# Expert weights in 19 fixed slots, loaded by one, two and four tiles, and the last expert finished as rows

## The chip, the cores and the metric

The kernel runs on one core of one Trainium2 chip. The metric is the device time of one execution in microseconds. Before the change it is 2363.58 us, the median of 3 runs (2362.69 to 2364.72).

## The reference

Two transformer blocks work on the same 512 tokens of width 1024. The first is a retention block with a convolutional FFN. The second is a gated-MLP and window-attention block that ends in an expert-choice FFN and a final norm. Nearly all of the change lies in that FFN and that norm:

```python
def expert_choice_ffn(h, w_router, w_gate, w_up, w_down):      # 16 experts, D = 1024, D_EXPERT = 2048
    logits = jnp.einsum('bnd,de->bne', h, w_router)
    aff = jax.nn.softmax(logits, axis=-1)
    top_w, top_idx = lax.top_k(jnp.swapaxes(aff, 1, 2), cap)   # each expert takes cap = 64 of 512 tokens
    xe = jax.vmap(lambda hb, ib: hb[ib])(h, top_idx)
    g = jnp.einsum('becd,edf->becf', xe, w_gate)
    u = jnp.einsum('becd,edf->becf', xe, w_up)
    y = jnp.einsum('becf,efd->becd', jax.nn.silu(g) * u, w_down)
    y = y * top_w[..., None].astype(y.dtype)
    ... # add each y to its token
# second_block:  x = x + g2 * expert_choice_ffn(h2, ...);  return rmsnorm(x, final_g)
```

All values are float32. The three weight matrices of an expert are 24 MiB, those of 16 experts 384 MiB.

## The kernel before

The first three fifths of the span compute the first block and the attention part of the second with dense matmuls, whose weights are split into a high and a low part (lines 222 to 224). The expert phase comes after them; there the weights are used as they are.

**Tiles and their order.** The 24 MiB of one expert are 24 tiles of 1 MiB, each 128 partitions by 2048 floats, a row of 8 KB in every partition. Each tile is one contiguous piece of the input `w_exp` of shape (16, 24, 128, 2048). Tiles 0 to 7 hold gate and up weights of the first half of the hidden width (`j = 0`), 8 to 15 those of the second (`j = 1`), 16 to 23 the down weights. TensorE takes four matmuls for each tile (line 1733 for gate and up, 1791 for down), with the expert's 64 tokens as the stationary operand. The tiles are numbered through, expert e beginning at 24e, so the last is 383.

**Buffers.** 22 tiles are loaded ahead (`FIRST`, `ORDER`, line 1448). 17 of them lie in rotating buffers of three pools (`xw0` 9, `xw1` 2, `xw2` 6), which are the ring that all later tiles go round. Two lie in ring buffers of the dense part (kind 4), and one each in `xw3`, in small buffers of the norms (kind 5), and in `hTe` with two more (kind 6). `XOUT` says how many of them are issued at which of the eight output columns of the last dense product; the last eight follow when the dense buffers are closed (`dense_stack.close()`).

**Loads.** `x_dma_to` (line 1464) issues one load of 1 MiB per tile on SyncE's queue. `x_ahead(used)` is called after every tile that TensorE's code has used, and issues each load whose buffer's former tile is below `used`. Each load waits on the chip for the last matmul on that buffer.

**Between the tiles.** In expert e, during `j = 0`, the 64 output rows of expert e-1 are added into the 512 rows of the residual (`scatter`, line 1690: a one-hot matmul into a bank `ps`, then VectorE adds it into `xacc`). After every second expert the tokens of the next two are gathered (line 1666).

**The end.** For expert 15 the down weights lie in another order: tiles 376 to 379 hold the first 512 output columns and 380 to 383 the second 512. `down` (line 1819) runs them one half after the other; between its tiles an identity matmul (line 1835) copies the residual's second half into four banks. The first half's rows are scaled (`scaled`, line 1827) and scattered (line 1841) after four of the eight tiles, the second half's after the last (line 1854). Then ScalarE squares and sums each row (line 1858), `rsqrt_` (line 326) gives the norm, the rows are scaled (lines 1868, 1869), and eight stores of 256 KB each (line 1871) write the output.

Of the kernel before, what the change touches and what calls it, by code (L numbers as in the profile page):

```python
# [9 lines left out]
F32 = mybir.dt.float32  # L10
# [7 lines left out]
L = 512  # L18
# [24 lines left out]
def block_kernel(ctx: ExitStack, tc: tile.TileContext, A, out):  # L43
# [307 lines left out]
    class SumSq:  # L351
        def __init__(self, n, tag):
# [181 lines left out]
    def ctx_norm(cx, cH, cL, a, b):  # L534

        ss = SumSq(256, "c")
# [30 lines left out]
    c1 = ctx_norm(cx, cH, cL, A1[:, :, 1:2], mod1[:, 0:8, 1:2])  # L567
# [487 lines left out]
    for j in range(HID):  # L1055
# [404 lines left out]
    def x_dma_to(n):  # L1460
        while wn["d"] < min(n, len(wq)):
            i = wn["d"]
            at = ORDER[i] if i < NFIRST else i
            e, t = wq[at]
            g = FIRST[i if i < NFIRST else RING[(i - NFIRST) % NRING]]
            src = A["w_exp"][e, t]
            if g > 3:
                if g == 4:
                    w = [b.bitcast(F32) for _ in range(2) for b in ring(True)]
                elif g == 5:  # L1470
                    w = soon + [mp.tile([128, L], F32, name="xf", tag="ssqa", bufs=1)]
                else:
                    h = xp.tile([128, 2, L], F32, name="hTe", tag="hTe", bufs=1)
                    w = [h[:, 0], h[:, 1]] + [mp.tile([128, L], F32, name="xf", tag="t2", bufs=2) for _ in range(2)]
                for c in range(3 if g == 5 else 0, 4):
                    nc.sync.dma_start(w[c], src[:, c * 512:(c + 1) * 512])
            else:
                w = xws[g].tile([128, 2048], F32, name=f"xw{g}", tag="xw", bufs=FIRST.count(g))
                for c in (slice(0, 1024), slice(1024, 2048)) if i == len(wq) - 1 else (slice(0, 2048),):
                    nc.sync.dma_start(w[:, c], src[:, c])  # L1480
                w = [w[:, c:c + 512] for c in range(0, 2048, 512)]
            wt[at] = w
            wn["d"] += 1
# [23 lines left out]
    xws.append(ctx.enter_context(tc.tile_pool(name="xw1", bufs=1, side="right")))  # L1507
# [13 lines left out]
    XOUT = (3, 4, 5, 6, 8, 10, 12, 13)  # L1521
# [20 lines left out]
    def epi_out2(j, ps):  # L1542
# [158 lines left out]
    fg = []  # L1701

    def final_gain(hf):
# [5 lines left out]
        fg.append(mp.tile([128, 512], F32, name="fg", tag="ssqb" if hf else "ssqa", bufs=1))  # L1709
        nc.vector.tensor_copy(fg[hf], p)  # L1710

    turns_e = []
    for e in range(NEXP):
# [10 lines left out]
        for j in range(2):  # L1724
            pgu = [pbank("pgu", 3), pbank("pgu", 3)]
            for n in range(8):
# [51 lines left out]
        S = mp.tile([128, L], F32, name="S", tag="nh", bufs=2).bitcast(F32R)  # L1778
        nc.vector.tensor_scalar(S, iota, sw[:, e:e + 1], None, OP.is_equal)
        if e == NEXP - 1:  # L1780
            final_gain(1)
            break
# [13 lines left out]
        if e == 0:  # L1796
# [3 lines left out]
            g2L = yp.tile([128, 2, 512], F32, name="g2L")  # L1800
# [6 lines left out]


    ssf = xp.tile([128, 2, 4], F32, name="ssf")
    nc.scalar.activation(ssf[:, 0, 0:1], ones, AF.Sqrt)  # L1810
    vf = xp.tile([128, 2, 4], F32, name="vf")

    def down(py, q):
        t = wt.pop(ti + q)
        for n in range(4):
            f = q % 4 * 4 + n
            rows = slice(64 * (n % 2), 64 * (n % 2) + 64)
            c = f % 4 * 128 + f // 4 % 2 * 64
            nc.tensor.matmul(py[rows, :], hTe[:, f // 8, c:c + 64],  # L1819
                             t[n], start=f < 2, stop=f > 13, skip_group_check=True)  # L1820
        x_ahead(ti + q + 1)

    def scaled(py, hf):
        yh = yp.tile([128, 512], F32R, name="yh", tag="yh", bufs=1)
        y32 = mp.tile([128, 512], F32, name="y32", tag="nh", bufs=2)
        yl = yp.tile([128, 512], F32R, name="yl", tag="yl", bufs=1)
        nc.vector.scalar_tensor_tensor(y32, py, sw[:, 31:32], g2L[:, hf], OP.mult, OP.mult)
        split(yh, yl, y32)
        return yh, yl
    py = [pbank("py", 2) for hf in range(2)]  # L1830
    xlast = []
    for q in range(4):
        down(py[0], q)
        xlast.append(pbank("pT", 1) if q == 3 else pbank("pgu", 3))
        nc.tensor.matmul(xlast[q], ident, xacc[q][1], start=True, stop=False)
    ys = scaled(py[0], 0)
    down(py[1], 4)
    for t in range(4):
        p = pbank("ps", 2)
        for y in ys:  # L1840
            nc.tensor.matmul(p, S[:, t * 128:(t + 1) * 128], y, start=y is ys[0], stop=y is ys[1])
        x = xacc[t][0]
        nc.vector.tensor_tensor(x, p, x, OP.add)
        sq = mp.tile([128, 512], F32, name="sqf", tag="t2", bufs=2)
        nc.scalar.activation(sq, x, AF.Square, accum_out=ssf[:, 0, t:t + 1])  # L1845
        nc.gpsimd.tensor_tensor(x, x, fg[0], OP.mult)  # L1846
    nc.vector.tensor_scalar(vf[:, 0], ssf[:, 0], 1.0 / D, EPS, OP.mult, OP.add)
    down(py[1], 5)
    down(py[1], 6)
    down(py[1], 7)  # L1850
    ys = scaled(py[1], 1)
    for y in ys:
        for t in range(4):
            nc.tensor.matmul(xlast[t], S[:, t * 128:(t + 1) * 128], y, start=False, stop=y is ys[1])
    def squares(ts):
        for t in ts:
            sq = mp.tile([128, 512], F32, name="sqf", tag="t2", bufs=2)
            nc.scalar.activation(sq, xlast[t], AF.Square, accum_out=ssf[:, 1, t:t + 1])

    def last_rms(g):  # L1860
        ts = slice(2 * g, 2 * g + 2)
        nc.vector.scalar_tensor_tensor(vf[:, 1, ts], ssf[:, 1, ts], 1.0 / D, vf[:, 0, ts], OP.mult, OP.add)
        return rsqrt_(vf[:, 1, ts], 2, "f" if g else "x")

    def finish(g, rf):
        for i in range(2):
            t = 2 * g + i
            nc.scalar.activation(xacc[t][0], xacc[t][0], AF.Copy, scale=rf[:, i:i + 1])
            nc.vector.scalar_tensor_tensor(xacc[t][1], xlast[t], rf[:, i:i + 1], fg[1], OP.mult, OP.mult)
            for hf in range(2):  # L1870
                nc.sync.dma_start(out[t * 128:(t + 1) * 128, hf * 512:(hf + 1) * 512], xacc[t][hf])
# [159 lines left out]
```

## Time and profile before

| | us |
|---|---|
| median of 3 runs | 2363.58 |
| the profiled execution | 2362.11 |
| its span, first to last instruction | 2360.3 |
| TensorE matmul busy in the span | 2237.4 |
| expert phase, from the first matmul of line 1733 | 1423.5 to 2360.3 |

The span is what the profile shows; the profiled execution's own time is 1.8 us longer. "PE" is TensorE, "DVE" VectorE, "ACT" ScalarE, "POOL" GpSimd and "SP" SyncE, which issues most loads. "DMA share" is the mean busy share of the core's 16 DMA engines; it can come out a little above 1. [...]

### The profile page before, as it was taken

What the parts mean: (1) busy time and instruction counts of PE and PEld (TensorE: products, weight loads), DVE (VectorE), ACT (ScalarE), POOL (GpSimd) and SP (SyncE); (2) the same over time, 40 slices, a digit from 0 to 9 for tenths busy, and PEclk for the clock granted to TensorE, in tenths of its full rate; (3) what the DMA queues carried; (4) which work ended last, traced back from release to release, by engine and by line L of the source; (5) the groups of instructions that cost most, each with busy time, mean ns of one, the idle gap of its engine ahead of it and who ended that gap; (6) DMA issues with size and microseconds to landing.
All of it is one profiled execution on the core that took longest, in us unless ns stands there. A gap on an engine that the chain in (4) does not pass through costs nothing.

```text
span 2360.3 us, 28316 instructions
## 1 busy us (share of the span) xinstructions
PE 2237.4 (95%) x11052; PEld 1441.4 (61%) x11052; DVE 1062.8 (45%) x2059; ACT 658.0 (28%) x1033; POOL 173.5 (7%) x318
## 2 busy tenths in 40 slices
PE   9999999999999999999999999999898989898987
PEld 6888888878888887888876874434232323232322
DVE  4645775778787865436467551221111111111112
ACT  5632234354243454322566321000000000000002
POOL 0201001101112010004211000000000000000000
PEclk9999999999999999999999999999999999999999
DMA  8646345734566443347410788999999999999996
GB/s 316 241 162 202 99 138 179 241 122 143 165 189 219 143 148 107 92 127 178 101 41 6 234 350 346 420 420 420 421 420 421 420 420 421 420 420 420 420 421 277
DMA packets 128725, 616.56 MB, mean 261 GB/s; under 512 B 16464, under 2 KB 21200, under 8 KB 79248
## 3 DMA queue, kind: packets, MB, share of 16 engines
q1 hardware_dynamic: 109200, 557.59, 61.3%
q0 software_dynamic: 19392, 57.17, 8.5%
q8 instruction: 87, 1.43, 0.2%
q14 instruction: 46, 0.38, 0.0%
HBM read 590.05 MB, written 14.68 MB: 256 GB/s over the span
## 4 chain that ended last, share of the span: by engine, by line
PE 53%; DMA 30%; ACT 2%; DVE 2%; issue 1%; POOL 0%; SPq 0%; DVEq 0%; ACTq 0%; POOLq 0%
DMA xw<-in_w_exp_dram 27%; PE mm L224 10%; PE mm L222 10%; PE mm L223 10%; PE pgu L1733 6%; PE py L1791 3%; PE sm L1358 1%; PE mm L1346 1%; PE ps L1666 1%; PE pT L1666 1%; PE py L1819 1%; DMA qS<-rh 1%; PE b L1309 1%; PE b L255 1%; PE b L253 1%
## 5 line engine op out<-in xcount | busy, mean ns | idle before, releaser
L1733 PE MATMUL pgu<-xw,xt 128*64 128x512 f32 x2032 | 480.6, 601 | 56.8 <-DMA xw<-in_w_exp_dram 52.6
L222 PE MATMUL mm<-aH,wh 128*128 128x512 f32 (+1 forms) x1104 | 420.1, 381 | 2.3 <-ACT aH L380 2.3
L224 PE MATMUL mm<-aH,wl 128*128 128x512 f32 (+1 forms) x1104 | 417.3, 378 | 1.0 <-DVE wl L131 1.0
L223 PE MATMUL mm<-aL,wh 128*128 128x512 f32 (+1 forms) x1104 | 417.5, 378 | 0.0
L1733 PEld LDWEIGHTS pgu<-xw,xt 128*64 128x64 f32 x2032 | 131.3, 136 | 354.9 <-issue 199.2
L131 DVE TENSOR_TENSOR wl<-wraw,wh 128x1024 fp32r<-128x1024 f32 (+1 forms) x212 | 256.2, 1212 | 177.3 <-ACT wh L122 177.1
L122 ACT ACTIVATE wh<-wraw 128x1024 fp32r<-128x1024 f32 (+1 forms) x212 | 220.0, 1044 | 254.0 <-PE mm L223 180.3
L222 PEld LDWEIGHTS mm<-aH,wh 128*128 128x128 f32 x1104 | 208.5, 189 | 40.8 <-ACT aH L380 2.6
L224 PEld LDWEIGHTS mm<-aH,wl 128*128 128x128 f32 x1104 | 208.4, 189 | 40.4 <-DVE wl L131 1.8
L1791 PE MATMUL py<-xw,hTe 128*64 128x512 f32 x944 | 214.7, 597 | 19.1 <-DMA xw<-in_w_exp_dram 19.1
L223 PEld LDWEIGHTS mm<-aL,wh 128*128 128x128 f32 x1104 | 208.5, 189 | 38.0 <-DVE aL L383 0.4
L1791 PEld LDWEIGHTS py<-xw,hTe 128*64 128x64 f32 x944 | 65.0, 136 | 157.4 <-issue 111.0
L1761 DVE TENSOR_TENSOR eg<-pgu,eg 128x512 f32<-128x512 f32 x32 | 22.1, 692 | 252.4 <-PE pgu L1733 243.1
L1804 DVE SCALAR_TENSOR_TENSOR y<-py,sw,g2B 128x512 f32<-128x512 f32 x15 | 11.3, 751 | 221.4 <-PE py L1791 221.4
L1723 ACT ACTIVATE hTe<-pT 128x512 f32<-128x512 f32 x32 | 19.1, 597 | 312.3 <-PE pT L1722 312.3
L1699 DVE TENSOR_TENSOR aH<-ps,aH 128x512 f32<-128x512 f32 x56 | 38.7, 692 | 124.1 <-PE ps L1696 124.1
L108 ACT ACTIVATE yh<-y 128x512 fp32r<-128x512 f32 x17 | 10.7, 630 | 253.9 <-DVE y L1804 239.1
L1846 POOL TENSOR_TENSOR aH<-aH,fg 128x512 f32<-128x512 f32 x4 | 5.0, 1284 | 1035.9 <-ACT sqf L1845 1035.9
L282 POOL DMA_DIRECT2D mraw<-in_w_adaT_dram x96 | 51.6, 537 | 304.9 <-DVE mod L297 302.6
L1760 ACT ACTIVATE eg<-pgu 128x512 f32<-128x512 f32 x32 | 19.1, 597 | 177.8 <-PE pgu L1733 177.8
L222 PE MATMUL mm<-gH,wh 128*128 128x512 f32 x176 | 68.5, 389 | 0.0
L223 PE MATMUL mm<-gL,wh 128*128 128x512 f32 x176 | 68.5, 389 | 0.0
(489 smaller groups left out, 3162.5 us busy)
## 6 DMA issues: line engine op xcount, KB each, us to landing
xw<-in_w_exp_dram SPq DMA_DIRECT2D x379, 1024.0 KB, 19.9
mraw<-in_w_adaT_dram POOLq DMA_DIRECT2D x96, 256.0 KB, 3.0
wraw<-in_w_up_dram SPq DMA_DIRECT2D x44, 512.0 KB, 3.9
wraw<-in_w_kv_tok_dram SPq DMA_DIRECT2D x20, 512.0 KB, 4.2
wraw<-in_w_bg_dram SPq DMA_DIRECT2D x16, 512.0 KB, 3.7
mraw<-in_w_modT_dram POOLq DMA_DIRECT2D x32, 256.0 KB, 4.5
mraw<-in_w_modT_dram SPq DMA_DIRECT2D x32, 256.0 KB, 4.1
wraw<-in_w_out_dram SPq DMA_DIRECT2D x16, 512.0 KB, 4.5
```

Of the source, the lines that this page charges most:

```text
L122: nc.scalar.activation(h[:, :sz], r[:, :sz], AF.Copy)
L131: nc.vector.tensor_tensor(*lows.pop(0), OP.subtract)
L222: nc.tensor.matmul(ps, wh, xh, start=first, stop=False)
L223: nc.tensor.matmul(ps, wh, xl, start=False, stop=False)
L224: nc.tensor.matmul(ps, wl, xh, start=False, stop=last)
L253: nc.tensor.matmul(ps[t][:, :cols], xh[:, ts], wh[:, s], start=k == 0, stop=False)
L255: nc.tensor.matmul(ps[t][:, :cols], xh[:, ts], wl[:, s], start=False, stop=k == KD - 1)
L282: eng.dma_start(t, A["w_modT" if b == 1 else "w_adaT"][c, hf])
L1666: nc.tensor.matmul(pT[:, c * 128:(c + 1) * 128], xtok[:, t, k * 128:(k + 1) * 128], sel[:, t], start=t == 0, stop=t == 3)
L1699: nc.vector.tensor_tensor(x, p, x if e else xtok[:, t, c], OP.add)
L1733: nc.tensor.matmul(pgu[w][64 * i:64 * i + 64, :], xt[:, kq, es], t[2 * k + i], start=kq == 0, stop=kq == 7, skip_group_check=True)
L1791: nc.tensor.matmul(py[64 * hf:64 * hf + 64, :], lhs, t[2 * i + hf], start=f8 == 0 and i == 0, stop=f8 == 7 and i == 1, skip_group_check=True)
```

## The change

The 24 tiles of an expert get another layout: `w_exp` has the shape (16, 6, 128, 8192), so that four consecutive tiles lie side by side in a row of 32 KB of each partition. Expert 15 has the common layout too.

The ring is 19 fixed slots of 8 KB per partition, in three regions of 9, 4 and 6 slots. 24 tiles are issued ahead instead of 22; `xw1` holds four of them instead of two. The later tiles go to slots by a written list. Tiles 24 to 47 are loads of one tile, 48 to 71 of two neighbours, 72 to 359 of four (72 loads, in the slots 13 to 16, 0 to 3, 4 to 7 and 9 to 12 in turn), 360 to 371 of two, and 372 to 383 of one. A load is issued once the last of the tiles that its slots held has been used.

The last expert is not scattered. While its gate and up tiles run, a one-hot matmul picks its 64 tokens' rows out of the residual (`last_pick`, `last_rows`). All 512 rows are squared, normed and scaled without expert 15's share (`most_squares`, `most_rms`, `most_finish`), and the eight stores write them (`most_store`). After its down tiles, which run as those of every other expert, its 64 rows are finished as 128 half rows of 512 floats, and one indirect store from GpSimd writes them over the rows in the output.

```diff
-            self.acc = mp.tile([128, n], F32, name="ssq", tag="ssq" + tag, bufs=1)
+            self.acc = (pool or mp).tile([128, n], F32, name="ssq", tag="ssq" + tag, bufs=1)
...
-    FIRST = [0] * 9 + [4] * 2 + [1] * 2 + [2] * 6 + [3, 5, 6]
-    ORDER = [0, 1, 2, 3, 4, 5, 6, 8, 9, 20, 21, 10, 11, 12, 13, 15, 16, 17, 18, 19, 14, 7]
+    SLOTS = [(0, i) for i in range(9)] + [(1, i) for i in range(4)] + [(2, i) for i in range(6)]
+    FIRST = [(i, s) for s, i in enumerate((0, 1, 2, 3, 4, 5, 6, 8, 9))] + [(10 + s, 9 + s) for s in range(4)]
+    FIRST += [(22, "k"), (23, "k")] + [(t, 13 + s) for s, t in enumerate((15, 16, 17, 18, 19, 20))]
+    FIRST += [(21, "e"), (14, "s"), (7, "h")]
+    units = [((i,), s) for i, s in FIRST]
+    units += [((i,), (i - 24) % NS) for i in range(24, 48)]
+    units += [((48 + 2 * i, 49 + 2 * i), s) for i, s in enumerate((5, 7, 9, 11, 13, 15, 17, 0, 2, 5, 7, 9))]
+    QUADS = (13, 0, 4, 9)
+    units += [(tuple(range(i, i + 4)), QUADS[i // 4 % 4 - 2]) for i in range(72, 360, 4)]
+    PAIRS = (13, 15, 0, 2, 4, 6, 9, 11)
+    units += [((i, i + 1), PAIRS[i // 2 % 8 - 4]) for i in range(360, 372, 2)]
+    units += [((i,), PAIRS[i // 2 % 8 - 4] + i % 2) for i in range(372, 384)]
...
+    holds, needs = {}, []
+    for u, s in units:
+        at = [s + n for n in range(len(u))] if isinstance(s, int) else []
...
+        needs.append(max([holds.get(n, -1) for n in at] + [-1]))
+        holds.update(zip(at, u))
...
+    def x_unit():
+        u, s = units[wn["u"]]
+        e, t = wq[u[0]]
+        src = A["w_exp"][e, t // 4][:, t % 4 * 2048:t % 4 * 2048 + 2048 * len(u)]
...
+                w = xregs[reg][:, at * 2048:(at + len(u)) * 2048]
+            for c in (slice(0, 1024), slice(1024, 2048)) if wn["u"] == len(units) - 1 else (slice(0, n),):
+                nc.sync.dma_start(w[:, c], src[:, c])
...
     def x_ahead(used):
-        while wn["d"] < NFIRST or wn["d"] < len(wq) and before(wn["d"]) < used:
-            x_dma_to(wn["d"] + 1)
+        while wn["u"] < len(units) and (wn["d"] < NFIRST or needs[wn["u"]] < used):
+            x_unit()
...
-    XOUT = (3, 4, 5, 6, 8, 10, 12, 13)
+    XOUT = (3, 5, 7, 9, 11, 13, 14, 15)
...
+    def last_rows():
+        xg = pbank("py", 2)
+        for t in range(4):
+            for hf in range(2):
+                nc.tensor.matmul(xg[64 * hf:64 * hf + 64, :], sel[:, t, 64:128], xacc[t][hf],
+                                 start=t == 0, stop=t == 3, skip_group_check=True)
...
+    def most_finish(t):
+        for hf in range(2):
+            nc.vector.scalar_tensor_tensor(xacc[t][hf], xacc[t][hf], fin_["r"][:, t:t + 1], fg[:, hf],
+                                           OP.mult, OP.mult)
+    def most_store():
+        for t in range(4):
+            for hf in range(2):
+                nc.sync.dma_start(out[t * 128:(t + 1) * 128, hf * 512:(hf + 1) * 512], xacc[t][hf])
...
+                if e == 10 and j == 0 and n > 5:
+                    final_gain(n - 6)
+                if e == NEXP - 1:
+                    if j == 0 and n == 6:
+                        last_pick()
+                        most_squares(0)
+                        most_squares(1)
+                    if j == 0 and n == 7:
+                        last_rows()
+                        most_squares(2)
+                        most_squares(3)
+                    if j == 1 and n == 1:
+                        most_rms()
+                    if j == 1 and 1 < n < 6:
+                        most_finish(n - 2)
+                    if j == 1 and n == 6:
+                        most_store()
...
-    py = [pbank("py", 2) for hf in range(2)]
...
-    squares((0, 1))
-    rf = last_rms(0)
-    squares((2, 3))
-    finish(0, rf)
-    finish(1, last_rms(1))
+    for i in range(2):
+        c = slice(256 * i, 256 * i + 256)
+        nc.vector.scalar_tensor_tensor(z[:, c], py[:, c], sw[:, 31:32], g2B[:, c], OP.mult, OP.mult)
+        nc.vector.tensor_tensor(z[:, c], fin_["xg"][:, c], z[:, c], OP.add)
+        sq = mp.tile([128, 512], F32, name="sqf", tag="t2", bufs=2)
+        nc.scalar.activation(sq[:, :256], z[:, c], AF.Square, accum_out=zs[:, i:i + 1])
+        for hf in range(2):
+            nc.tensor.matmul(ps[64 * hf:64 * hf + 64, 0:1], sel[:, 0, 0:64], zs[:, i:i + 1],
+                             start=i == 0, stop=i == 1, skip_group_check=True)
+        nc.gpsimd.tensor_tensor(z[:, c], z[:, c], fin_["fgB"][:, c], OP.mult)
+    nc.vector.tensor_scalar(vz, ps[:, 0:1], 1.0 / D, EPS, OP.mult, OP.add)
+    rz = rsqrt_(vz, 1, "f")
+    nc.scalar.activation(z[:, 0:256], z[:, 0:256], AF.Copy, scale=rz)
+    nc.vector.tensor_scalar(z[:, 256:512], z[:, 256:512], rz, None, OP.mult)
+    nc.gpsimd.indirect_dma_start(out.rearrange("t (h c) -> (t h) c", h=2),
+                                 bass.IndirectOffsetOnAxis(ap=fin_["row"], axis=0), z, None)
...
-    A["w_exp"] = np.ascontiguousarray(w.reshape(16, 12, 128, 2, 2048).transpose(0, 1, 3, 2, 4)).reshape(16, 24, 128, 2048)
-    A["w_exp"][15, 16:] = d[15].reshape(4, 4, 128, 2, 512).transpose(3, 0, 2, 1, 4).reshape(8, 128, 2048)
+    A["w_exp"] = np.ascontiguousarray(w.reshape(16, 6, 2, 128, 4096).transpose(0, 1, 3, 2, 4)).reshape(16, 6, 128, 8192)
```

## Rows read from the trace of the kernel before

**Rows 1.** Windows by stretch: busy us of each engine, PEclk, DMA share, GB/s.

```profile
2200.00:2300.00 100.00, 88.33 (x426) 31.18 (x426) 17.43 (x29) 5.75 (x11) 0.00 (x0) 1.00 1.01 420
```

**Rows 2.** What TensorE waited for, 1400 to 2361 us: us, times, longest.

```profile
PE pgu L1733 <- DMA xw<-in_w_exp_dram: 52.6, 100, 0.8
PE py L1791 <- DMA xw<-in_w_exp_dram: 19.1, 36, 0.7
```

**Rows 3.** The chain of waits: start us, us, what.

```profile
1423.54 7.02 PE pgu L1733 x32
...
1513.13 13.88 PE py L1791 x64
1527.02 5.15 PE pgu L1733 x24
...
1548.05 10.47 PE pgu L1733 x48
...
1560.02 13.88 PE py L1791 x64
...
1627.79 5.15 PE pgu L1733 x24
...
2319.16 1.96 PE pgu L1733 x8
...
2345.20 0.76 DVE y L1827
```

**Rows 4.** Windows before the first expert and at the end, columns as in 1.

```profile
1391.00:1398.00 7.00, 7.00 (x40) 6.01 (x40) 2.33 (x4) 1.16 (x2) 0.00 (x0) 1.00 0.11 37
...
1402.00:1403.00 1.00, 0.00 (x0) 0.00 (x0) 0.82 (x4) 0.87 (x2) 0.00 (x0) 0.50 1.04 442
...
1421.00:1426.00 5.00, 5.00 (x39) 3.23 (x40) 0.19 (x1) 2.90 (x5) 0.00 (x0) 0.99 0.02 6
...
2338.00:2339.00 1.00, 0.68 (x3) 0.30 (x2) 1.00 (x2) 0.44 (x1) 0.00 (x0) 1.00 0.11 45
```

**Rows 5.** DMA queues, 1700 to 2300 us: packets, MB, share of 16 engines.

```profile
DMA packets 34605, 252.18 MB, mean 420 GB/s; under 512 B 3843, under 2 KB 3843, under 8 KB 3843
...
q1 hardware_dynamic: 34579, 251.80, 101.1%
...
xw<-in_w_exp_dram SPq DMA_DIRECT2D x239, 1024.0 KB, 19.9
```

**Rows 6.** DMA queues, 10 to 40 us.

```profile
DMA packets 3211, 12.24 MB, mean 408 GB/s; under 512 B 356, under 2 KB 356, under 8 KB 3081
...
q1 hardware_dynamic: 3209, 12.21, 101.4%
```

**Rows 7.** DMA queues, 2351 to 2360 us, the stores of the output.

```profile
q1 hardware_dynamic: 1152, 2.10, 63.1%
```

**Rows 8.** DMA queues, 139.5 to 142.5 us, the one load of 16 KB rows.

```profile
q1 hardware_dynamic: 64, 1.05, 91.6%
```

**Rows 9.** DMA issues of the whole span: KB each, median us to landing.

```profile
xres<-in_xT_dram POOLq DMA_DIRECT2D x4, 512.0 KB, 7.7
x_d<-xres POOLq DMA_DIRECT2D x8, 256.0 KB, 3.0
```

**Rows 10.** Timeline of the end: start us, us, engine, line, operation.

```profile
2337.78 1.29 DVE L1843 TENSOR_TENSOR aH<-ps,aH 128x512 f32<-128x512 f32 x2 [1.38 <-PE ps L1841]
...
2348.79 0.59 ACT L1858 ACTIVATE sqf<-pgu 128x512 f32<-128x512 f32 x1
2349.26 0.20 ACT L1858 ACTIVATION_READ_ACCUMULATOR sqf<-pgu 128x1 f32 x1
2349.50 0.16 DVE L1862 SCALAR_TENSOR_TENSOR vf<-ssf,vf 128x2 f32<-128x2 f32 x1 [2.16 <-ACT sqf L1858]
...
2350.72 1.41 DVE L1869 SCALAR_TENSOR_TENSOR aL<-pgu,rs,fg 128x512 f32<-128x512 f32 x2
...
2355.55 0.60 SPq L1871 DMA_DIRECT2D out_dram<-aL  x1
```

More of the change, by code (lines that the diff above doesn't have):

```diff
@@ L1456, in block_kernel @@
+    assert [i for u, _ in units[NFIRST:] for i in u] == list(range(24, 384))
+    holds, needs = {}, []
+    for u, s in units:
+        at = [s + n for n in range(len(u))] if isinstance(s, int) else []
+        assert len({SLOTS[n][0] for n in at}) < 2
+        needs.append(max([holds.get(n, -1) for n in at] + [-1]))
+        holds.update(zip(at, u))
     wt = {}
     soon = []
-    wn = {"d": 0}
+    wn = {"u": 0, "d": 0}
+    def x_unit():
+        u, s = units[wn["u"]]
+        e, t = wq[u[0]]
+        src = A["w_exp"][e, t // 4][:, t % 4 * 2048:t % 4 * 2048 + 2048 * len(u)]
+        if isinstance(s, int) or s == "e":
+            if s == "e":
+                w = xearly[0]
+            else:
+                reg, at = SLOTS[s]
+                w = xregs[reg][:, at * 2048:(at + len(u)) * 2048]
+            n = 2048 * len(u)
+            for c in (slice(0, 1024), slice(1024, 2048)) if wn["u"] == len(units) - 1 else (slice(0, n),):
+                nc.sync.dma_start(w[:, c], src[:, c])
+            w = [w[:, c:c + 512] for c in range(0, n, 512)]
+        else:
+            if s == "k":
+                w = [b.bitcast(F32) for _ in range(2) for b in ring(True)]
+            elif s == "s":
+                w = soon + [mp.tile([128, L], F32, name="xf", tag="ssqa", bufs=1)]
+            else:
+                h = xp.tile([128, 2, L], F32, name="hTe", tag="hTe", bufs=1)
+                w = [h[:, 0], h[:, 1]] + [mp.tile([128, L], F32, name="xf", tag="t2", bufs=2) for _ in range(2)]
+            for c in range(3 if s == "s" else 0, 4):
+                nc.sync.dma_start(w[c], src[:, c * 512:(c + 1) * 512])
+        for n, i in enumerate(u):
+            wt[i] = w[4 * n:4 * n + 4]
+        wn["u"] += 1
+        wn["d"] += len(u)
@@ L1460, in x_dma_to @@
     def x_dma_to(n):
         while wn["d"] < min(n, len(wq)):
[L1462 to L1481, printed above, removed]
@@ L1708, in final_gain, with last_pick @@
                              start=True, stop=True)
-        fg.append(mp.tile([128, 512], F32, name="fg", tag="ssqb" if hf else "ssqa", bufs=1))
-        nc.vector.tensor_copy(fg[hf], p)
+        nc.scalar.activation(fg[:, hf], p, AF.Copy)
+    ssf = xp.tile([128, 2, 4], F32, name="ssf")
+    fin_ = {}
+    def last_pick():
+        p = pbank("ps", 2)
+        nc.tensor.matmul(p[:, :64], ident[0:16, 15:16].to_broadcast([16, 128]), idx, start=True, stop=True)
+        for t in range(4):
+            nc.vector.tensor_scalar(sel[:, t, 64:128], p[:, :64], V("tok")[:, t:t + 1], None, OP.is_equal)
+        nc.gpsimd.tensor_tensor(sel[:, 0, 0:64], ident[:, 0:64], ident[:, 64:128], OP.add)
@@ new lines, in last_rows @@
+    def last_rows():
[4 more added lines that the diff above has]
+                                 start=t == 0, stop=t == 3, skip_group_check=True)
+        fin_["xg"] = xg
+        rowf = xp.tile([128, 2], F32, name="rowf")
+        nc.vector.tensor_scalar(rowf[:, 0:1], V("tok")[:, 0:1], 64.0, None, OP.is_ge)
+        nc.vector.scalar_tensor_tensor(rowf[:, 1:2], sw[:, 15:16], 2.0, rowf[:, 0:1], OP.mult, OP.add)
+        fin_["row"] = xp.tile([128, 1], U32, name="row")
+        nc.vector.tensor_copy(fin_["row"], rowf[:, 1:2])
+        fgB = mp.tile([128, 512], F32, name="fgB", tag="ssqb", bufs=1)
+        for hf in range(2):
+            nc.gpsimd.tensor_copy(fgB[64 * hf:64 * hf + 64], fg[64 * hf:64 * hf + 64, hf])
+        fin_["fgB"] = fgB
@@ L1712, in block_kernel @@
+    def most_store():
+        for t in range(4):
+            for hf in range(2):
+                nc.sync.dma_start(out[t * 128:(t + 1) * 128, hf * 512:(hf + 1) * 512], xacc[t][hf])
     turns_e = []
@@ L1777, in block_kernel @@
             nc.scalar.activation(g2B, p, AF.Copy)
[L1778 to L1782, printed above, removed]
+        if e < NEXP - 1:
+            S = mp.tile([128, L], F32, name="S", tag="nh", bufs=2).bitcast(F32R)
+            nc.vector.tensor_scalar(S, iota, sw[:, e:e + 1], None, OP.is_equal)
+        else:
+            nc.scalar.activation(ssf[:, 1, 0:1], ones, AF.Sqrt)
         py = pbank("py", 2)
@@ L1799, in block_kernel @@
             xacc = [[b.bitcast(F32) for b in ring(True)] for t in range(4)]
[L1800 removed]
+            fg = yp.tile([128, 2, 512], F32, name="fg")
+        if e == NEXP - 1:
+            break
         yh = yp.tile([128, 512], F32R, name="yh", tag="yh", bufs=1)
@@ L1806, in block_kernel @@
         pend.append((e, yh, yl, S))
[L1809 to L1829, printed above, removed]
-    py = [pbank("py", 2) for hf in range(2)]
[L1831 to L1835, printed above, removed]
@@ L1848, in block_kernel @@
[L1848 to L1863, printed above, removed]
@@ L1865, in finish @@
[L1865 to L1871, printed above, removed]
-    squares((0, 1))
-    rf = last_rms(0)
-    squares((2, 3))
-    finish(0, rf)
-    finish(1, last_rms(1))
+    z = mp.tile([128, 512], F32, name="y32", tag="nh", bufs=2)
@@ new lines, in block_kernel @@
+    zs = xp.tile([128, 2], F32, name="zs")
+    vz = xp.tile([128, 1], F32, name="vz")
+    ps = pbank("ps", 2)
+    for i in range(2):
+        c = slice(256 * i, 256 * i + 256)
+        nc.vector.scalar_tensor_tensor(z[:, c], py[:, c], sw[:, 31:32], g2B[:, c], OP.mult, OP.mult)
+        nc.vector.tensor_tensor(z[:, c], fin_["xg"][:, c], z[:, c], OP.add)
+        sq = mp.tile([128, 512], F32, name="sqf", tag="t2", bufs=2)
+        nc.scalar.activation(sq[:, :256], z[:, c], AF.Square, accum_out=zs[:, i:i + 1])
+        for hf in range(2):
+            nc.tensor.matmul(ps[64 * hf:64 * hf + 64, 0:1], sel[:, 0, 0:64], zs[:, i:i + 1],
+                             start=i == 0, stop=i == 1, skip_group_check=True)
+        nc.gpsimd.tensor_tensor(z[:, c], z[:, c], fin_["fgB"][:, c], OP.mult)
```

60 lines of the change are left out of this document (22 added, 38 removed).

## The prediction

> **What bounds the kernel now.** I read the windows by stretch first. Late in the expert phase the 16 DMA engines are busy for 1.01 of the time at 420 GB/s, while TensorE is busy for 88.3 of 100 us at full clock [rows 1]: the loads set the pace. The waits say how much a faster stream could give at most: TensorE stood 52.6 + 19.1 = 71.7 us for weights [rows 2]. The DMA queues give the price of a tile: 251.80 MB in 600 us are 2.50 us per MiB, and 19.9 us from issue to landing are eight of these, so eight loads are on their way at any time [rows 5]. The chain of waits gives TensorE's own pace while it is still behind the loads: from 1527.02 to 1627.79 two experts, 100.8 us for 48 tiles or 2.10 us each; a tile alone takes 7.02 / 4 = 1.76 us [rows 3]. The windows before the first expert show the engines nearly idle at 1391 to 1398 and 1421 to 1426 us, and the last weights arriving at about 2338.6 us [rows 4]. TensorE ends its down tiles 6.6 us later, at 2345.2 [rows 3], and 15.1 us more pass until the span ends at 2360.3.
>
> So the end time is the start of the stream, plus its bytes at its rate, plus its idle spots, plus what follows the last weights. The change touches all four.
>
> **1. Two more tiles ahead.** Their 2.1 MB need 5.0 us at 420 GB/s, and 1391 to 1398 holds 7 us in which only 37 GB/s flowed [rows 4]. They are issued earlier on SP's queue, ahead of the last two weight loads of the dense product, which then land up to two tiles (5.0 us) later; these weights are fetched and split several columns ahead of their use, which hides it. When the first expert starts, 360 tiles are left instead of 362: -5.0 us. If that cover were too short, TensorE would start later by as much as is won: the ends are -5.0 and 0.
>
> **2. Coarser slots.** A load of two or four waits for the last of the tiles that it replaces, with all later loads behind it on SP and TensorE waiting for those in the end. Tile 0 is used at 1423.54 + 1.76 = 1425.3 and data flow from 1426 [rows 3, 4], so about 1 us passes from release to data. Loads 24 to 57 would be through at 1426.5 + 34 x 2.50 = 1511.5; the next pair needs tile 40, the first of eight down tiles from 1513.13, done at 1514.9. Tiles 24 to 71 would be through at 1546.5 plus that wait; the first load of four needs tile 59, second of the six from 1548.05, done at 1551.5. The next needs tile 65, second of the eight from 1560.02, done at 1563.5, about 1 us after the load before it [all rows 3]. That is 1 to 3 us of idle engines three times, some 7 us, against about 2 us that the kernel before loses to waits of one tile (estimated: the same kind of release, one at a time). I take +5; the ends are 0 and +9. Later there is nothing: a quad's slots are refilled while three quads (30 us of loads) are ahead, and TensorE needs 4 x 2.10 = 8.4 us for what takes 10 us to load. If TensorE needed more than that, this cover would be gone.
>
> **3. Longer rows.** The packets are the rows of a partition. An 8 KB row took 1.011 x 600 x 16 / (34579 - 3843) us = 315.8 ns of an engine [rows 5]. A 4 KB row took (1.014 x 30 x 16 - 128 x 0.316) / (3081 - 356) us = 163.8 ns [rows 6], a 2 KB row of the output stores 0.631 x 9 x 16 / 1024 us = 88.7 ns [rows 7] (the small packets counted as nothing). From 2 to 4 KB that is 37.6 ns per KB, from 4 to 8 KB 38.0, and some 12 ns are left that each row costs whatever its length. A 32 KB row would then take 315.8 + 24 x 38.0 = 1228 ns against 4 x 315.8 = 1263. An engine has 8 rows of each load: 35 ns x 8 x 72 loads of four = 20.4 us, and 12 ns x 8 x 18 loads of two = 1.7 us; over the share of 1.011 that is -22 us. With 37.6 ns per KB it would be -27. The other end has one row: the only load with 16 KB rows took 0.916 x 3 x 16 / 64 us = 687 ns a row, more than 2 x 315.8 = 632 [rows 8]. I don't take it: the engines were not full then, and three sizes lie on a line. If rows are cut back to 8 KB, the term is 0.
>
> [...]
>
> **4. TensorE behind the last weights.** Before, it had 26 us of work from 2319.16, identity matmuls and a scatter among it, for eight tiles that come in 20 us; hence the 6.6 us. After, only half a tile (0.9 us) and the landing (about 1) follow the last weights: 2.0, so -4.6. For that TensorE must have caught up. From the landing of the last load of four, loads need 6 x 4.9 + 12 x 2.50 = 59.4 us; TensorE needs four tiles (7.0), an expert with scatter (1527.02 to 1573.9, 46.9) and the eight matmuls that pick rows (two tiles' worth, 3.5) [rows 3]: 57.4. The margin is thin; ends -5 and 0.
>
> [...] With loads of four it stands up to 9.7 - 7.0 = 2.7 us at a time instead of 0.8 [rows 2]. [...]
>
> **5. After the last matmul.** Scaling takes 0.75 us for 512 columns [rows 3], adding 1.29 / 2, and an operation on two columns 0.16 [rows 10]. Halves are so about 0.45 and 0.40, two of each 1.7 us. The square and its sum take 0.4 + 0.2; the one-column matmul has no row of its own, I put 0.4; from 2349.50 to 2350.72 the norm takes 1.2; the scaling of halves 0.4; hand-overs 0.3 [rows 10]. That is 4.6 us. GpSimd's products lie beside the norm. The trace has no indirect store; the nearest row is GpSimd's store of the same 256 KB in 2 KB rows, 3.0 us, the farthest its loads of 512 KB, 7.7 [rows 9]. I take 3.0. Before, the last store was issued at 2355.55 [rows 10]; with 3.0 to land, 1.7 us remain to the end. So 9.3 instead of 15.1: -5.8. The eight plain stores (5.7 us of the engines [rows 7]) stand behind the last weights on SP's queue and run beside this chain: they are through some 6 us after the last weights, when the half rows are ready (2.0 + 4.6). I take -5.5. Ends: -6, and with 7.7 us for the store -1; were the stores ahead of the last weights, +5.7 on top.
>
> The squares, products and picks of the other rows lie on engines that idle through the expert phase (VectorE busy 17.4, ScalarE 5.8 of 100 us [rows 1]), and the norms' buffers only change place: nothing.
>
> **Sum.** -5.0 + 5 - 22 - 4.6 - 5.5 = -32 us on the profiled execution's 2362.1: 2330. The median of the runs lies 1.5 us above that execution, so 2332.
>
> **Rivals.**
> - *A, the forecast*, 2332 (2324 to 2342 by the ends of terms 1, 2, 4 and 5): 62%.
> - *B, the rows are cut to 8 KB or cost by the byte alone.* For it: nothing in the trace has 32 KB rows. Against it: 16 KB packets exist [rows 8]. Term 3 is 0: 2363.6 - 10.1 = 2353. 17%.
> [...]
> - *D, slower: long rows leave the engines waiting*, as rows 8 have it. At 687 ns per 16 KB a 32 KB row takes 1374 ns, 111 more than four short ones: 111 x 8 x 72 and 55 x 8 x 18, over 1.011, are +71 us, with the other terms 2424. It decides from 18 ns more per row (10.1 us over 8 x 72), that is from 1281 ns. For it is that one load, against it the line through three sizes. 9%.
> - *E, the idle spots cost +9, nothing is gained by term 1, B holds, and the indirect store takes 7.7 us*: 0 + 9 - 4.6 - 1 = +3, 2367. 5%.
>
> **How the numbers follow.** A measurement of this kernel can tell a change of about 0.2%, 4.7 us, from none. A, B and C are faster by more: 86%. E is within: 5%. D is slower: 9%. The range reaches from A's low end to B: 2324 to 2354.
>
> **What would show it.** [...] Packets of 32 KB at 1228 ns. Idle engines near 1515, 1552 and 1564 us, none after 1600. TensorE's waits in fewer, longer pieces, 50 us or more in sum, at PEclk 1.00. The last weights at about 2317, the last down matmul 2 us behind them, the end 11 us behind them. A stream that isn't full after 1600, a TensorE that is more than 4 us behind at the end, or an indirect store over 5 us would make single terms wrong; only term 3 could turn the sign.

## The result and the profile after

The changed kernel takes 2333.93 us (median of four runs, 2332.93 to 2334.41) against 2363.87 us: a ratio of 0.9873, with a 95% interval of 0.9856 to 0.9890. The profiled execution took 2332.93 us, of it a span of 2331.2 us, 29.1 less than before.

The DMA queues of the changed kernel, 1700 to 2250 us (packets, MB, share of 16 engines; then issues, KB each, us to landing), answer to [rows 5]:

```profile
DMA packets 8165, 237.29 MB, mean 431 GB/s; under 512 B 911, under 2 KB 911, under 8 KB 911
...
q1 hardware_dynamic: 8142, 236.95, 100.1%
...
xr<-in_w_exp_dram SPq DMA_DIRECT2D x55, 4096.0 KB, 30.8
```

The stream runs at 431 GB/s instead of 420. A 32 KB row takes 1.001 x 550 x 16 / (8142 - 911) = 1218 ns of an engine; I had forecast 1228.

Windows of the changed kernel (columns as in rows 1; PEclk is the granted TensorE clock as a share of its full speed), answering to [rows 4] and [rows 1]:

```profile
1391.00:1398.00 7.00, 7.00 (x40) 6.01 (x40) 2.16 (x4) 1.29 (x3) 0.00 (x0) 1.00 0.56 207
...
1515.00:1516.00 1.00, 1.00 (x8) 0.35 (x6) 0.00 (x0) 0.00 (x0) 0.00 (x0) 1.00 0.12 49
1551.00:1552.00 1.00, 1.00 (x8) 0.31 (x6) 0.00 (x0) 0.23 (x1) 0.00 (x0) 1.00 0.12 49
1563.00:1564.00 1.00, 1.00 (x8) 0.34 (x6) 0.00 (x0) 0.00 (x0) 0.00 (x0) 1.00 0.01 0
...
1791.00:1794.00 3.00, 2.71 (x8) 0.98 (x10) 0.00 (x0) 0.00 (x0) 0.00 (x0) 0.50 1.11 481
...
1700.00:2250.00 550.00, 490.04 (x2386) 191.19 (x2382) 91.12 (x161) 37.51 (x70) 1.00 (x3) 0.98 1.00 431
```

The two tiles more fill part of the gap before the first expert (207 GB/s where 37 flowed), and the three idle spots stand where the chain of waits had put them. The last row has the granted clock at 0.98, not 1.00: in parts of the stretch TensorE is granted less, in 1791 to 1794 0.50. What it waited for, 1450 us to the end (us, times, longest), answers to [rows 2]:

```profile
PE pgu L1805 <- DMA xr<-in_w_exp_dram: 47.1, 38, 2.5
PE py L1871 <- DMA xr<-in_w_exp_dram: 21.4, 16, 2.7
```

Nearly the same sum as before (68.5 us for 71.7), in 54 pieces instead of 136 and up to 2.7 us long: the loads still set the pace.

The timeline of the end (start us, us, engine, line, operation) answers to [rows 10]:

```profile
2317.90 3.65 PE L1871 MATMUL py<-xr,hTe 128*64 128x512 f32 x16 [0.56 <-DMA xr<-in_w_exp_dram]
...
2320.45 0.22 PEld L1871 LDWEIGHTS py<-xr,hTe 128*64 128x64 f32 x4 [0.64 <-DMA xr<-in_w_exp_dram]
2320.47 0.33 SPq L1782 DMA_DIRECT2D out_dram<-aL  x1
2321.61 0.48 DVE L1895 SCALAR_TENSOR_TENSOR y<-py,sw,g2B 128x256 f32<-128x256 f32 x1 [17.81 <-PE py L1871]
...
2324.32 0.16 DVE L1903 TENSOR_SCALAR vz<-ps 128x1 f32<-128x1 f32 x1 [0.93 <-PE ps L1900]
...
2325.59 0.51 ACT L1905 ACTIVATE y<-y,rs 128x256 f32<-128x256 f32 x1 [0.87 <-DVE rs L330]
...
2326.84 1.07 POOL L1907 DMA_INDIRECT out_dram<-y,row  x1 [2.10 <-ACT y L1905]
```

The last weights are there at 2320.4 (forecast 2317), the last down matmuls end at 2321.6, and the span ends at 2331.2, 10.8 us after the last weights (forecast 11). The old end had 21.3: the last weights landed at 2339.05 in the trace of before, and the span ended at 2360.3. So 10.5 us of the 29.1 are the end's, and the last weights come 18.6 earlier (forecast: 22).

### The profile page after: what moved, and what is told of

The parts are those of the page before. It is cut to its first block, busy times and chain, and to the rows that moved or that the text cites. A ratio compares the mean times of both kernels' runs of the same rounds, so it can differ in the third digit from the quotient of the medians.

```text
span 2331.2 us, 27830 instructions
## 1 busy us (share of the span) xinstructions
PE 2222.0 (95%) x11038; PEld 1461.5 (63%) x11038; DVE 1060.8 (46%) x2064; ACT 658.3 (28%) x1034; POOL 172.8 (7%) x320
## 4 chain that ended last, share of the span: by engine, by line
PE 70%; DMA 25%; DVE 2%; ACT 1%; issue 1%; POOL 1%; POOLq 0%; DVEq 0%; SPq 0%; ACTq 0%
DMA xr<-in_w_exp_dram 23%; PE mm L222 12%; PE mm L224 12%; PE mm L223 12%; PE pgu L1805 9%; PE py L1871 4%; PE b L255 2%; PE b L254 2%; PE b L253 2%; PE sm L1358 1%; PE mm L1346 1%; DMA qS<-rh 1%; PE b L222 1%; PE b L223 1%; PE b L224 1%
## 5 line engine op out<-in xcount | busy, mean ns | idle before, releaser
L1805 PE MATMUL pgu<-xr,xt 128*64 128x512 f32 x2032 | 467.3, 602 | 48.4 <-DMA xr<-in_w_exp_dram 47.1
L1805 PEld LDWEIGHTS pgu<-xr,xt 128*64 128x64 f32 x2032 | 144.8, 138 | 317.9 <-issue 265.7
L1871 PE MATMUL py<-xr,hTe 128*64 128x512 f32 x1008 | 229.1, 609 | 21.4 <-DMA xr<-in_w_exp_dram 21.4
L1871 PEld LDWEIGHTS py<-xr,hTe 128*64 128x64 f32 x1008 | 75.3, 140 | 163.9 <-issue 150.3
L222 PE MATMUL mm<-gH,wh 128*128 128x512 f32 x176 | 68.5, 389 | 0.0
L223 PE MATMUL mm<-gL,wh 128*128 128x512 f32 x176 | 68.5, 389 | 0.0
L224 PE MATMUL mm<-gH,wl 128*128 128x512 f32 x176 | 68.5, 389 | 0.0
```

The costliest lines, as they stand in the source:

```text
L222: nc.tensor.matmul(ps, wh, xh, start=first, stop=False)
L223: nc.tensor.matmul(ps, wh, xl, start=False, stop=False)
L224: nc.tensor.matmul(ps, wl, xh, start=False, stop=last)
L1805: nc.tensor.matmul(pgu[w][64 * i:64 * i + 64, :], xt[:, kq, es], t[2 * k + i], start=kq == 0, stop=kq == 7, skip_group_check=True)
L1871: nc.tensor.matmul(py[64 * hf:64 * hf + 64, :], lhs, t[2 * i + hf], start=f8 == 0 and i == 0, stop=f8 == 7 and i == 1, skip_group_check=True)
```

## The experiments

They ran in sets, each set on one chip beside the kernel before, whose median there is given; the first four are one set, the others lie on a second chip. Each line of a diff is against the changed kernel unless it says otherwise.

**Each load of two or four cut into loads of one**

```diff
- ... else (slice(0, n),):
+ ... else [slice(b, b + 2048) for b in range(0, n, 2048)]:
```

> Each load of two or four tiles is issued as that many loads of one tile, with 8 KB rows again; slots, order and what each load waits for stay as in the changed kernel. Theory (the 20 us of the loads come from the longer rows): 2333.9 + 72 x 0.276 + 18 x 0.1 = +21.7, so 2354 to 2356, packets of 8 KB at about 316 ns and a stream of 420 GB/s. Rival (the gain comes from something else, such as the fixed slots or fewer waits on semaphores): within 4 us of the changed kernel, 2330 to 2338, with the stream still near 431 GB/s.

Measured: 2343.26 us, ratio 0.9913 (0.9898 to 0.9928), before 2363.57. Neither theory: only 9 us come back of the 22, though the stream is back at 422 GB/s. One reason is the wait: each of the smaller loads waits for its own tile alone, so this undoes the coarse waits too, other than the expectation says. The window with two of the idle spots (columns as in rows 1) is full here, where the changed kernel has 349 GB/s (shown below):

```profile
1550.00:1575.00 25.00, 24.14 (x116) 8.15 (x114) 2.32 (x4) 1.82 (x3) 0.00 (x0) 1.00 1.01 423
```

The next run keeps the coarse waits.

**Loads of four with 8 KB rows**

```diff
+ src = A["w_exp"][e, t:t + m].rearrange("m p c -> p m c")
+ w3 = w.rearrange("p (m c) -> p m c", m=m)
- A["w_exp"] = ....reshape(16, 6, 128, 8192)
+ A["w_exp"] = ....reshape(16, 24, 128, 2048)
```

> The loads stay of one, two and four tiles, but the weights lie tile by tile in memory as before, so that a load of four is 512 rows of 8 KB instead of 128 of 32 KB. Theory (row length): 2354 to 2356, as when each load is split, and 8 KB packets at about 316 ns. Rival (the number and size of the loads matter, 175 fewer issues and completions): 2332 to 2338.

Measured: 2349.84 us, ratio 0.9942 (0.9929 to 0.9956), before 2363.57. 16 us come back of the 20 to 22 expected, so it is row length in the main, and not the number of loads (there are as few as in the changed kernel). But 8 KB rows ran at 423 GB/s here against 420 before. Of every four loads of four, one landed 9.72 us behind the load before it and the others 9.96: always the one in the same slots, 13 to 16.

**The new end alone, with the old loads**

```diff
+ FIRST, ORDER, RING, x_dma_to, x_ahead: as in the kernel before (22 tiles ahead, loads of one)
```

> The loads are the old ones (one tile each, 22 ahead, no fixed slots); only the last expert's rows and the end after the last weights are the new ones. Theory (the end and the loads add): the last weights land where they did before (2339), the span ends 10.5 us earlier: 2363.9 - 10.5 = 2353.4 (2351 to 2356). Rival (the shorter end depends on the new loads, or the new work of the last expert holds the last loads up): 2358 to 2366.

Measured: 2346.79 us, ratio 0.9926 (0.9912 to 0.9939), before 2363.57: 16.8 less, where 10.5 were expected. The end did what it should: the last weights' matmuls begin at 2335.68 and the span ends at 2346.4, 10.7 us later.

```profile
2335.68 0.23 PEld L1848 LDWEIGHTS py<-xw,hTe 128*64 128x64 f32 x4 [0.63 <-DMA xw<-in_w_exp_dram]
```

But the old loads had become faster too. Its DMA queues, 1700 to 2250 us:

```profile
DMA packets 31944, 232.80 MB, mean 423 GB/s; under 512 B 3546, under 2 KB 3546, under 8 KB 3546
...
q1 hardware_dynamic: 31920, 232.45, 101.0%
```

These are loads that nobody touched, and a row takes 1.010 x 550 x 16 / (31920 - 3546) = 313.2 ns. What differs is where the slots lie. In the program as built, all slots before begin 32 bytes past a multiple of 64 (48800, 121888, 138272 and steps of 8192: six 160 bytes past a multiple of 256, eleven 32 past one); the diff takes a buffer of 1 KB per partition (that of `ctx_norm`) out of a pool below slots 13 to 18 and adds some small ones, which moves these six from 48800 to 47872, a multiple of 256. That gave the new theory: the start address of a row counts. Below, a slot is well placed if it begins at a multiple of 256, and badly placed if not. The changed kernel has six well placed slots (13 to 18) and thirteen badly placed ones.

**Slots taken by age**

```diff
- units += [((i,), (i - 24) % NS) ...], QUADS, PAIRS
+ def by_age(i, n):   # the run of n neighbours whose youngest tile is the oldest
+     best = min((max(last_in[q] for q in range(p, p + n)), ..., p) for ...)
+ for n in [1] * 38 + [2] * 7 + [4] * 71 + [2] * 6 + [1] * 12: at_ = by_age(at_, n)
```

> The changed kernel, but after the first 24 each load takes the run of neighbouring slots whose last tile is the oldest, with 38 loads of one, 7 of two, 71 of four, 6 of two and 12 of one. Theory (the two tiles gained at the start are lost again because a load of two or four waits for its youngest slot, in idle spots near 1515, 1551 and 1563 of some 8 us together): those spots go or shrink, 2326 to 2330. Rival (the idle spots come from the bound of how many tiles fit, whatever slots are taken): 2332 to 2336.

Measured: 2328.94 us, ratio 0.9849 (0.9835 to 0.9862), before 2363.57, 5.0 us less than the changed kernel. The same 25 us (1550 to 1575), first of the kernel before, then of the changed kernel, then of this one:

```profile
1550.00:1575.00 25.00, 24.14 (x114) 8.09 (x112) 1.84 (x3) 1.39 (x3) 0.00 (x0) 1.00 1.02 422
```

```profile
1550.00:1575.00 25.00, 24.14 (x115) 8.09 (x112) 1.83 (x3) 1.32 (x3) 0.00 (x0) 1.00 0.86 349
```

```profile
1550.00:1575.00 25.00, 24.13 (x114) 8.09 (x112) 2.21 (x4) 1.82 (x3) 0.00 (x0) 1.00 1.02 437
```

The idle spots are gone, as the first theory said. The 88 GB/s that the changed kernel misses in these 25 us are 2.2 MB, 5.1 us of the stream at 431 GB/s. The list also has 14 more loads of one tile at its start, so the 5.0 us are those of the whole list and not of the order alone.

**The kernel before, with only its slots' addresses moved** (diff against before)

```diff
+ ctx.enter_context(tc.tile_pool(name="pad0", bufs=1, side="right")).tile([128, 8], F32, name="pad0")
+ ctx.enter_context(tc.tile_pool(name="pad2", bufs=1)).tile([128, 24], F32, name="pad2")
```

> The kernel before with nothing but the addresses of its slots moved: 32 bytes per partition are left out above the slots on the right side and 96 below those on the left, so that every slot begins at a multiple of 256 bytes instead of 32 bytes past a multiple of 64. New theory (the start address of a row sets the rate, not its length; in the run with loads of four as 8 KB rows, the one group of four slots that begins at a multiple of 256 took 9.72 us a load and the other three 9.96): every load 2.43 us instead of 2.49, 362 x 0.06 = -21.7, less what TensorE can't free in time around 1500 to 1600: 2342 to 2348. Rival (that group of slots is faster for another reason, such as the side of the memory, or longer rows are needed): 2360 to 2364.

Measured: 2349.76 us, ratio 0.9948 (0.9934 to 0.9962), before 2362.25. The address alone is worth 12.5 us, without one instruction changed. But that is less than the 16 to 21 expected. Its DMA queues, 1700 to 2250 us:

```profile
DMA packets 32202, 234.68 MB, mean 427 GB/s; under 512 B 3575, under 2 KB 3575, under 8 KB 3575
...
q1 hardware_dynamic: 32177, 234.32, 100.9%
```

An 8 KB row now takes 1.009 x 550 x 16 / (32177 - 3575) = 310.4 ns instead of 315.8, and the stream runs at 427 GB/s, not at the 431 of 32 KB rows. Read by their landings in a stream with slots of both kinds, the one group of well placed slots had looked as fast as that; when all are well placed, a tile takes 1.0486 MB / 427 = 2.456 us, not 2.43. So address and length each have a part.

**Other offsets** (diff against before)

```diff
+ pad0 of 224 bytes (nine slots 64 past a multiple of 256), pad1 of 192 (two slots 128 past), pad2 of 96 (six at 0)
```

> The kernel before with its slots at three offsets: nine slots 64 bytes past a multiple of 256, two 128 past, six at a multiple of 256. If any multiple of 64 is enough, all loads take 2.43 us and the time is that of the run with all at 256 (2342 to 2348). If a multiple of 256 is wanted, eleven of seventeen loads keep 2.49 us and the time is 2363.6 - 21.7 x 6/17 = 2356 (2354 to 2359).

Measured: 2354.32 us, ratio 0.9965 (0.9951 to 0.9978), before 2362.25: 7.9 less, with 5.2 to 11.6 by the interval. Its DMA queues, 1700 to 2250 us:

```profile
DMA packets 32028, 233.41 MB, mean 424 GB/s; under 512 B 3555, under 2 KB 3555, under 8 KB 3555
...
q1 hardware_dynamic: 32004, 233.07, 101.0%
```

The expectation for a multiple of 256 holds by its number, but it went by the 21.7 us that the run before has put at 12.5; of these, six slots in seventeen are 4.4. So 64 and 128 past may have a part of the gain. The rows say how much: 1.010 x 550 x 16 / (32004 - 3555) = 312.4 ns, against 313.2 with the same six slots well placed and the others 32 past (the new end with the old loads) and 310.4 with all well placed. Put on the eleven other slots alone, that is on average 4.3 ns a row at 32 past and 3.1 at 64 or 128 past: most of the cost stays there.

**Small loads, all slots at multiples of 256**

```diff
+ the cut into loads of one, and pad0 of 32 bytes
```

> The changed kernel with every load of two and four issued as loads of one tile (8 KB rows) and all slots at multiples of 256 bytes. Theory (address, not length): 2343.3 - 12/16 x 21 = about 2328 (2326 to 2331), and so faster than the changed kernel with its 32 KB rows. Rival (the row length carries the gain as I forecast, 0.07 us a tile): 2340 to 2344.

Measured: 2334.45 us, ratio 0.9880 (0.9865 to 0.9896), before 2362.25; the stream at 427 GB/s. It lies between the two theories: 8 KB rows, well placed, with waits of one tile, get as far as the changed kernel with 32 KB rows, thirteen of nineteen slots badly placed, and coarse waits, but not further.

**The changed kernel, its other thirteen slots moved**

```diff
+ pad0 of 32 bytes
```

> The changed kernel with its other thirteen slots moved by 32 bytes to multiples of 256. Its loads of four take 9.72 us on either kind of slot, so only the loads of one and two gain, some 30 x 0.06 = -2 us: 2331 to 2334. If the address still costs the long rows something, less: down to 2328.

Measured: 2331.15 us, ratio 0.9866 (0.9851 to 0.9881), before 2362.25, 2.8 us less than the changed kernel by the medians, as expected, though the intervals overlap. Its DMA queues, 1700 to 2250 us:

```profile
DMA packets 8180, 237.75 MB, mean 432 GB/s; under 512 B 912, under 2 KB 912, under 8 KB 912
...
q1 hardware_dynamic: 8157, 237.41, 100.1%
```

A 32 KB row takes 1215.8 ns.

**Rows of 16 KB**

```diff
- ... else (slice(0, n),):
+ ... else [slice(b, min(b + 4096, n)) for b in range(0, n, 4096)]:
+ pad0 of 32 bytes
```

> The changed kernel with each load of four issued as two loads of two (16 KB rows), all slots at multiples of 256 bytes. From the packets of 8 KB (309.4 ns) and 32 KB (1214.5 ns) on such slots, a row costs 7.7 ns beside its bytes, so one of 16 KB 611 ns and the stream 430 GB/s: 2334.5 - 4 to 5 for 288 tiles at 0.015 us less, and the waits are half as coarse as the changed kernel's: 2328 to 2331. If the length matters not at all beside the address: 2333 to 2336.

Measured: 2329.20 us, ratio 0.9854 (0.9839 to 0.9869), before 2363.76, as expected. Its DMA queues, 1700 to 2250 us:

```profile
DMA packets 16250, 236.72 MB, mean 430 GB/s; under 512 B 1800, under 2 KB 1800, under 8 KB 1800
...
q1 hardware_dynamic: 16226, 236.36, 100.5%
```

A 16 KB row takes 1.005 x 550 x 16 / (16226 - 1800) = 613.1 ns. Well placed rows of 8, 16 and 32 KB take 310.4, 613.1 and 1215.8 ns: two of 8 KB cost 7.7 ns more than one of 16, two of 16 10.4 more than one of 32. Some 8 to 10 ns a row are its own cost, and the bad start of an 8 KB row adds 5.4.

**22 tiles ahead**

```diff
- FIRST += [(22, "k"), (23, "k")] + ...
+ units += [((i,), (i - 22) % NS) for i in range(22, 48)]   # pairs shifted by one place
+ XOUT = (3, 5, 7, 9, 11, 13, 13, 13)
```

> The changed kernel with 22 tiles loaded ahead instead of 24; the loads of one go on from tile 22, the slots of the loads of two shift with them. Theory (the first two tiles more are lost again in the idle spots near 1515, 1551 and 1563, which shrink when the stream is two tiles later): 2333 to 2336. Rival (each tile ahead is worth its 2.5 us in full, as I forecast): 2338 to 2340.

Measured: 2332.24 us, ratio 0.9867 (0.9852 to 0.9882), before 2363.76: no slower than with 24. Windows of this run, before the first expert and at the three idle spots:

```profile
1391.00:1398.00 7.00, 7.00 (x39) 5.98 (x38) 2.10 (x3) 1.15 (x2) 0.00 (x0) 1.00 0.12 38
1515.00:1516.00 1.00, 1.00 (x8) 0.31 (x6) 0.83 (x3) 0.10 (x1) 0.00 (x0) 1.00 1.07 459
1551.00:1552.00 1.00, 1.00 (x8) 0.35 (x6) 0.00 (x0) 0.00 (x0) 0.00 (x0) 1.00 1.04 442
1563.00:1564.00 1.00, 1.00 (x8) 0.38 (x6) 0.00 (x0) 0.00 (x0) 0.00 (x0) 1.00 0.91 393
```

The gap of 1391 is open again and the idle spots are gone: with these slots, the time won ahead of the first expert is the time lost at 1515 to 1564.

**A plain store at the end**

```diff
- nc.gpsimd.indirect_dma_start(out.rearrange(...), bass.IndirectOffsetOnAxis(ap=fin_["row"], axis=0), z, None)
+ nc.gpsimd.dma_start(out.rearrange("t (h c) -> (t h) c", h=2)[0:128], z)
```

> The changed kernel with its last 128 half rows stored to fixed places in order, by a plain DMA of the same queue, instead of to the rows listed by the router (the output rows are others). In the trace the indirect store took 0.74 us to start, 1.07 us on GpSimd and some 2.5 us to its landing. Theory (the list costs the end what GpSimd takes to read it): 0.5 to 1.5 us less, 2332.4 to 2333.4. Rival (it hides behind the product on VectorE and ScalarE, or a plain one takes as long): 2333.5 to 2335.

Measured: 2331.50 us, ratio 0.9865 (0.9850 to 0.9880), before 2363.76. This kernel writes the rows to other places than the router's, to see what the list costs. The interval doesn't tell its time from the changed kernel's, and the 2.4 us between the medians are more than either theory had. The trace shows the step itself:

```profile
2325.16 0.51 ACT L1905 ACTIVATE y<-y,rs 128x256 f32<-128x256 f32 x1 [0.87 <-DVE rs L330]
...
2326.12 0.61 POOL L1907 DMA_DIRECT2D out_dram<-y  x1 [1.81 <-ACT y L1905]
```

From the end of the scaling to the end of the issue it takes 2326.73 - 2325.67 = 1.06 us, against 2327.91 - 2326.10 = 1.81 for the list. The list costs 0.75 us, as far as one trace of each shows it.

**Slots by age, all at multiples of 256**

```diff
+ by_age and pad0 of 32 bytes
```

> The kernel with slots taken by age, and all of them at multiples of 256 bytes. If the two gains add: 2328.9 - 2.8 (what the same shift gave the changed kernel) = 2326 (2324 to 2328). If TensorE is by now what bounds more of the time (it is busy for 2222 us), the shift gives less than 1 us: 2328 to 2330.

Measured: 2324.00 us (2322.07 to 2325.01), ratio 0.9832 (0.9818 to 0.9845), before 2363.76. It beats both kernels: its interval lies wholly below that of the changed kernel.

## Why the prediction was right

The forecast was 2332 us with a sum of -32; measured are 2333.93 and -29.9. Term by term:

1. **Two more tiles, -5.0, and coarser slots, +5.** Their sum of nothing holds (22 tiles ahead took 1.7 us less than 24, within the noise), and both sizes do. Small loads on well placed slots gained 27.8 us with 24 tiles and the new end, 12.5 with 22 tiles and the old end: 15.3 apart, of which the end has 10.5, so 4.8 for the two tiles. The coarse waits cost 5.0 us by the medians (2333.93 to 2328.94, with slots by age). What I had not seen is that the two are one thing: take the tiles away and the waits go too. With this order of slots the 24 tiles are worth nothing; with slots by age they should keep their worth, which no run with 22 tiles and slots by age shows.

2. **Longer rows, -22.** The size was right to some 3 us (the last weights come 18.6 us earlier, where terms 1 to 3 had 22), the sentence on its origin half right. Loads and waits unchanged, rows back at 8 KB, cost 15.9 us, not 22. The step that failed is under term 5: "the norms' buffers only change place: nothing". Moving one of them shifted six slots to a multiple of 256 bytes, so 8 KB rows in the changed kernel are no longer those of before. My 12 ns "that each row costs whatever its length", read from rows of 2, 4 and 8 KB, mix two costs: 8 to 10 ns of the row itself, and 5.4 for a badly placed start. A 32 KB row pays both once where four rows paid them four times (1218 ns as placed, 1215.8 with every slot at a multiple of 256), and so the sum came out without my knowing its parts; that much of it is luck. The parts by time: -12.5 us for the addresses alone (8 KB rows), and from there -12.0 for rows of 32 KB without idle spots (2334.45 to the 2324.00 of slots by age, each against its own before: -27.8 to -39.8).

   The cost of the start was no higher at 64 and 128 past a multiple of 256 (3.1 ns on average) than at 32 (4.3).

3. **TensorE behind the last weights, -4.6.** The half tile behind the last landing ended 1.2 us after it (2320.4 to 2321.6): at the forecast 2 us or a little better. The thin margin held.

4. **After the last matmul, -5.5.** From 2321.6 to the span's end it takes 9.6 us; I had 9.3. The unknown in it, the indirect store, took 1.8 us to its issue and 3.3 more to the end. The eight plain stores were no hindrance. They were issued from 2305.43 to 2320.47, behind the last load at 2303.0, and so their rows ran in part beside the last weights' rows and not behind them. The DMA queues from 2310 to 2319.9 us, when the last weights' rows are through:

```profile
DMA packets 1074, 3.67 MB, mean 371 GB/s; under 512 B 124, under 2 KB 124, under 8 KB 879
```

Of the 879 - 124 = 755 short rows, 256 are the 4 KB rows of the last tile, which is loaded in two halves; the other 499 are 2 KB rows of the stores, about half of their 1024. Yet the last load took as long from its issue to its landing as in the kernel before, where no store runs beside it (KB, us to landing; the kernel before, then this one):

```profile
xw<-in_w_exp_dram SPq DMA_DIRECT2D x1, 512.0 KB, 17.4
```

```profile
xr<-in_w_exp_dram SPq DMA_DIRECT2D x1, 512.0 KB, 17.4
```

The rivals: B (rows cut or cost by the byte) and D (long rows wait, 1374 ns) fall with 1218 ns. E needs B. No run shows a fixed cost of a quarter of my 12 ns a row, on which C and its 7 of the 86% stand: on well placed slots 8 to 10 ns are measured.

On the clock, I had written 1.00 between 1700 and 2250, which was wrong. With loads of four TensorE's 54 waits last 1.27 us on average, 2.7 at most, and the granted clock is 0.98; with rows of 16 KB there are 73 waits of 0.96 us on average, 2.6 at most, and it rounds to 1.00. The waits with rows of 16 KB (1450 us to the end), and the window of 1700 to 2250 us with them and in the fastest kernel:

```profile
PE pgu L1806 <- DMA xr<-in_w_exp_dram: 52.8, 55, 2.6
PE py L1872 <- DMA xr<-in_w_exp_dram: 17.6, 18, 1.3
```

```profile
1700.00:2250.00 550.00, 485.42 (x2380) 184.28 (x2380) 90.15 (x159) 37.55 (x70) 1.53 (x3) 1.00 1.01 430
```

```profile
1700.00:2250.00 550.00, 489.49 (x2390) 191.29 (x2388) 90.14 (x159) 37.59 (x70) 1.54 (x3) 0.98 1.00 432
```

The fastest kernel of all has 0.98 there too: the loads pace it (the DMA engines busy for 1.00 at 432 GB/s), and TensorE, busy for 489.5 of 550 us, has time to be slow. At the end of the changed kernel the clock was 1.00 (2317.9 to 2321.6 us), and the half tile behind the last weights took 1.2 us.

Open is why a group of well placed slots lands faster (9.72 us for four) between badly placed ones than when all are well placed (9.82), and how much of each term the chip adds: the medians of before lie 1.6 us apart between sets.

## What to carry to other kernels

When loads pace a kernel, divide a stretch's engine time by its packets: here the cost of a row that doesn't shrink with its length, some 12 ns by a fit over sizes, said within some 3 us what longer rows would bring, though such a fit gives the sum of all these costs without naming them. Look at the start address of every buffer that a DMA fills all the time, for paddings of 32 and 96 bytes were worth 12.5 us here, and a buffer moved elsewhere can shift it unseen. When loads are made coarser, let each take the slots that have been idle longest, or what is won ahead of the stream is handed back in waits (5.0 us here).

## What the runs showed that I had not expected

- The same 8 KB rows take 315.8 ns of a DMA engine when they start 32 bytes past a multiple of 64 in SBUF, and 310.4 at a multiple of 256: 420 against 427 GB/s.
- A kernel with nothing but its buffers moved ran 0.5% faster (0.9948, 0.9934 to 0.9962).
- An indirect store of 128 rows of 2 KB costs 0.75 us more to issue than a plain one of the same rows, in one trace of each.
